# Starting addresses and group lengths of split weights in a two-layer decoder trunk

## The chip, the cores and the metric

The kernel runs on one core of one Trainium2 chip. The metric is the time of one execution on the device, in microseconds: before the change 1123.68 us as the median of three runs (1123.16 to 1127.1).

## The reference: what is computed

A trunk of two decoder layers works on 256 tokens of width 1,024. Each layer, cut to what matters here:

```python
h = rms_norm(x, norm_mix_pre[l])
q, k, v, lru_x, lru_gate, glu_in, gate_logits = split(h @ w_in[l])
y_a = dilated_attention_mixer(q, k, v, cos, sin, w_o_attn[l])   # three groups of 8 heads, rotary q and k
y_b = rg_lru_mixer(lru_x, lru_gate, ...)                        # conv(4), scan, gelu gate, w_o_lru
y_c = conformer_conv_mixer(glu_in, ...)                         # GLU, conv(31), layer norm, w_o_conv
x = x + rms_norm((g0 * y_a + g1 * y_b + g2 * y_c) @ w_out[l], norm_mix_post[l])
u = square(relu(rms_norm(x, norm_mlp_pre[l]) @ w_mlp_up[l]))    # 1024 -> 4096
x = x + rms_norm(u @ w_mlp_down[l], norm_mlp_post[l])           # 4096 -> 1024
```

All of it is fp32. All the weights are used once, so some 200 MB of them pass through the core in one execution.

## The kernel before, in words

**Split matmuls.** A product of two fp32 matrices is made of three products of rounded parts (type fp32r): high by high, high weight by low activation, low weight by high activation. Names say which: `whi_`/`wlo_` are the high and low part of a weight chunk, `hh`/`hl` (also `uh`/`ul`, `yh`/`yl`, `zh`/`zl`, `oh`/`ol`, `mh`/`ml`) those of activations.

**Chunks.** The weights come as 92 chunks of 1 MB a layer (128 partitions by 2,048 fp32). `weights()` (L508) does one: a DMA on SP's queue into `raw` (ring of 2), a cast on ScalarE that makes `whi` (L416, two pieces of 1,024 columns), a subtraction on VectorE that makes `wlo` (L429, two pieces). `whi` and `wlo` are rings of three tiles each (`NHI`). `Shifted` puts the data some elements into its tile; `off` is that offset.

**Two kinds of use.** In a "ws" chunk the weights are loaded and 256 columns of activations (all tokens) move: glu, lx, lg, q, k, ga, gb, gc, oa, ob, oc and up. A half chunk is eight row blocks k of 128, so 16 matmuls on `whi` and 8 on `wlo`; a chunk has 48. In an "as" chunk the activations are loaded and 512 columns of weights move: v, wo (w_out), ua (the first part of up) and dn (down); a chunk has 24. The chunk dn61 of layer 0 is split into separate slots (`spread`) because it is used later.

**Order.** The program is a list of operations, put in order on each engine by a list scheduler (`Sched.run`) from costs, latencies and priorities. The `main` operations, which are groups of matmuls, follow each other on TensorE in the order of the table `ORDER`; all other work of TensorE (transposes `tp`, scores `sc`, attention output `pv`, norms) is put between two of them. So a group of matmuls that is one `main` operation is not interrupted. `ws_items` (L724) gives the matmuls of a half chunk in two groups, which `ws_mm` hands to `main`; `attn_out` (L1086) calls it with four row blocks rather than eight. The scores `sc` have one PSUM tile: a score operation waits until VectorE has taken masked maxima `mx` (L969) of the one before. All matmuls are issued at L476.

**Addresses.** They follow from the tile sizes. A tile of a weight ring is (2,048 + 32) x 4 = 8,320 bytes, which is 32 x 256 + 128. Going round the ring of three, the start of a tile within 256 bytes is 128 or 0 in turn. With the offset of 64 bytes (ws chunks, v1, v2) a chunk has its high part at 192 and its low part at 64, or the other way round; with offset 0 (the other as chunks) the two are at 128 and 0, or 0 and 128. The activations' parts and the slots of dn61 all start at 128.

Of the kernel before, what the change touches and what calls it, by code (L numbers as in the profile page):

```python
# [8 lines left out]
F32R = mybir.dt.float32r  # L9
# [4 lines left out]
P = 128  # L14
# [5 lines left out]
CHUNK = 2048  # L20
# [26 lines left out]
def chunk_plan():  # L47
    q0, k0, v0, lx0, lg0, gl0, br0 = 0, 1536, 3072, 4608, 5632, 6656, 8704
    plan = []

    def ws(name, mat, c0, c1=None):
        plan.append((name, "ws", mat, (c0, c0 + P if c1 is None else c1)))

    for n in ORDER:
        kind, a = n[:2], n[2:]
        if n[0] == "v":
            for kb in range(2):
                plan.append((f"{n}{kb}", "as", "w_in", (kb, v0 + int(n[1]) * 512)))
        elif n[0] in "qk":
            plan.append((n, "rope", "w_in", (q0 if n[0] == "q" else k0) + int(n[1]) * 512 + int(n[2]) * 256))  # L60
        elif kind == "gl":
            ws(n, "w_in", gl0 + int(n[3]) * P, gl0 + D + int(n[3]) * P)
        elif kind == "oa":
            plan.append((n, "oa", "w_o_attn", int(a) * 512))
        elif kind != "lw":
            mat, c0 = {"lx": ("w_in", lx0), "lg": ("w_in", lg0), "ga": ("w_in", br0), "gb": ("w_in", br0 + D),
                       "gc": ("w_in", br0 + 2 * D), "ob": ("w_o_lru", 0), "oc": ("w_o_conv", 0)}[kind]
            ws(n, mat, c0 + int(a) * 256)
    for c in range(2):
        for kb in range(2):  # L70
            plan.append((f"wo{c}{kb}", "as", "w_out", (kb, c * 512)))
    for kb in range(9):
        if kb == 0:
            plan += [(f"ua{k}", "as", "w_mlp_up", (k, 0)) for k in range(2)]
        elif kb < 8:
            ws(f"up{2 * kb}", "w_mlp_up", (2 * kb) * 256)
            ws(f"up{2 * kb + 1}", "w_mlp_up", (2 * kb + 1) * 256)
        if kb > 0:
            for c in range(2):
                plan.append((f"dn{kb - 1}{c}", "as", "w_mlp_down", (kb - 1, c * 512)))  # L80
    return plan
# [11 lines left out]
NHI = 3  # L93
# [10 lines left out]
LINE = 128  # L104
# [272 lines left out]
def trunk_kernel(ctx: ExitStack, tc: tile.TileContext, x_d, pos_d, w_d, lruw_d, par_d, gain_d, const_d, id_d, out_d):  # L377
    nc = tc.nc
    cp = ctx.enter_context(tc.tile_pool(name="cp", bufs=1))
    wp = ctx.enter_context(tc.tile_pool(name="wp", bufs=1))  # L380
    sp = ctx.enter_context(tc.tile_pool(name="sp", bufs=1))
    pp = ctx.enter_context(tc.tile_pool(name="pp", bufs=1, space=bass.MemoryType.PSUM))
    S = Sched()
# [4 lines left out]
    def slot(name, dt=F32, shape=(P, 2, T)):  # L388
        return S.buf(sp, shape, dt, "s2", name, NSLOT)
# [58 lines left out]
    def dma(eng, out, in_, nbytes):  # L448
        def fn():
            o = out.ap() if isinstance(out, View) else out  # L450
            i = in_.ap() if isinstance(in_, View) else in_
            eng.dma_start(out=o, in_=i)

        e = {id(nc.gpsimd): "POOL", id(nc.scalar): "ACT"}.get(id(eng), "SP")
        o = S.op(e, DMA_ISSUE[e], fn, views(in_), views(out))
        o.dma = nbytes / DMA_RATE / 1e3
        return o
# [40 lines left out]
    def split(hi, lo, src, scale=None):  # L498
        if scale is None:
            return act(hi, src, AF.Copy), tt(lo, src, hi.f32(), OP.subtract)  # L500
        return (act(hi, src, AF.Copy, scale=scale),
                stt(lo, src, scale, hi.f32(), OP.mult, OP.subtract))

    KIND = {p[0]: p[1] for p in chunk_plan()}
# [3 lines left out]
    def weights(l, name, spread=False):  # L508
        c = CIDX[name]
        assert c == used[l], (name, c, used[l])  # L510
        used[l] += 1
        nm = f"{name}_{l}"
        raw = S.buf(wp, (P, CHUNK), F32, "raw", f"raw_{nm}", NRAW)
        if l or c:
            o = dma(nc.sync, raw.all(), w_d[l * NCH + c], CHUNK * P * 4)
            if l == 0 and c in late:
                S.follow(o, late[c])
        else:
            for s in range(2):
                o = dma(nc.sync, raw[:, s * HALF:(s + 1) * HALF], w_d[0][:, s * HALF:(s + 1) * HALF], HALF * P * 4)  # L520
                if ORDER[0][0] == "v":
                    S.follow(o, x1_load)
        if spread:
            hs, ls = [], []
            for q in range(4):
                hs.append(slot(f"whi_{nm}{q}", F32R, (P, 512)))
                ls.append(slot(f"wlo_{nm}{q}", F32R, (P, 512)))
                for o in split(hs[q].all(), ls[q].all(), raw[:, q * 512:(q + 1) * 512]):
                    o.prep = True
            return [(Quarters(hs[2 * s:2 * s + 2]), Quarters(ls[2 * s:2 * s + 2])) for s in range(2)]  # L530
        off = 0 if KIND[name] == "as" and name[:2] not in ("v1", "v2") else LINE // 8
        hi = Shifted(S.buf(wp, (P, CHUNK + LINE // 4), F32R, "whi", f"whi_{nm}", NHI), off)
        lo = Shifted(S.buf(wp, (P, CHUNK + LINE // 4), F32R, "wlo", f"wlo_{nm}", NHI), off)
        n = HALF if l == 0 and c < 2 else PREP
        for b in range(0, CHUNK, n):
            for o in split(hi[:, b:b + n], lo[:, b:b + n], raw[:, b:b + n]):
                o.prep = True
        return [(Part(hi, s * HALF), Part(lo, s * HALF)) for s in range(2)]
# [184 lines left out]

    def ws_items(ps, j, w, rhs, nk=8, pitch=P, off=0):  # L724
        hi, lo = w
        a, b = [], []
        for k in range(nk):
            s = slice(k * pitch + off, k * pitch + off + P)
            mh, ml = rhs(k)
            a.append((ps[:, j, :], hi[:, s], mh, k == 0, False))  # L730
            a.append((ps[:, j, :], hi[:, s], ml, False, False))
            b.append((ps[:, j, :], lo[:, s], mh, False, k == nk - 1))
        return a, b

    def ws_mm(ps, w, rhs):
        first = last_main[0]
        for j in range(2):
            main(*ws_items(ps, j, w[j], rhs))

    for l in range(L):  # L740
# [49 lines left out]
        def glu(i):  # L790
            w = weights(l, f"glu{i}")
            ps = mm_ps(f"glu{i}_{l}")
            gemm(f"glu{i}", w, ps, hr)
            if i % 2 == 0:
                upad[i // 2] = S.buf(sp, (P, 2, 288), F32, "upad", f"upad{i}_{l}", 4)
                memset(upad[i // 2][:, :, 0:30], 0.0)
            u2 = upad[i // 2]
            th = slot(f"gth{i}_{l}", shape=(P, T))
            act(th.all(), ps[:, 1, :], AF.Tanh, scale=0.5)
            stt(u2[:, i % 2, 30:30 + T], th.all(), 1.0, ps[:, 0, :], OP.add, OP.mult)  # L800
            if i % 2 == 1:
                conv_pair(i // 2)
# [3 lines left out]
        def lx(j):  # L806
            w = weights(l, f"lx{j}")
            ps = mm_ps(f"lx{j}_{l}")
            gemm(f"lx{j}", w, ps, hr)
            xp = S.buf(sp, (P, 2, 260), F32, "xp", f"xp{j}_{l}", 2)  # L810
            memset(xp[:, :, 0:3], 0.0)
            act(xp[:, :, 3:3 + T], ps.all(), AF.Copy)
            u = slot(f"lu{j}_{l}")
            for s in range(2):
                i = 2 * j + s
                act(u[:, s, :], ps[:, s, :], AF.Identity, scale=p1(par, CW + 24 + i), bias=p1(par, CB + i))
            for k in range(3):
                for s in range(2):
                    i = 2 * j + s
                    stt(u[:, s, :], xp[:, s, k:k + T], p1(par, CW + k * 8 + i), u[:, s, :], OP.mult, OP.add)  # L820
            lu[j] = u
            luh[j] = slot(f"luh{j}_{l}", F32R)
            lul[j] = slot(f"lul{j}_{l}", F32R)
            split(luh[j].all(), lul[j].all(), u.all())
# [3 lines left out]
        def lg(j):  # L828
            w = weights(l, f"lg{j}")
            ps = mm_ps(f"lg{j}_{l}")  # L830
            gemm(f"lg{j}", w, ps, hr)
            q = slot(f"gq{j}_{l}")
            act(q.all(), ps.all(), AF.Square, scale=0.044715 ** 0.5)
            stt(q.all(), q.all(), 1.0, ps.all(), OP.add, OP.mult)
            act(q.all(), q.all(), AF.Tanh, scale=0.7978845608028654)
            g = slot(f"gel{j}_{l}")
            stt(g.all(), q.all(), 1.0, ps.all(), OP.add, OP.mult)
            gel[j] = g
# [247 lines left out]
        mh, ml = {}, {}  # L1086
# [23 lines left out]
        for name in ORDER:  # L1110
            kind, a = name[:2], name[2:]
# [46 lines left out]
        for t in range(2):  # L1158
            nm = f"pm{l}{t}"
# [82 lines left out]
        for t in range(2):  # L1242
            nm = f"pd{l}{t}"
# [100 lines left out]
```

## Time and profile before

| | before |
|---|---|
| median of three runs | 1123.68 us |
| the profiled execution, its own time | 1124.8 us |
| its span | 1123.0 us |
| TensorE busy (matmuls) | 1103.7 us, 98% |
| VectorE busy | 903.7 us, 80% |
| ScalarE busy | 726.0 us, 65% |
| GpSimd busy | 70.8 us, 6% |
| DMA, mean over the span | 187 GB/s |

The own time is that of the whole execution; the span runs from the first to the last instruction in the trace, and all points in time below count from its start. Busy time of matmuls is a sum over a pipelined engine whose ends are modelled: the duration of a single row (0.28 us) overlaps the next, so the pace is read from one start to the next, or from the chain, where a stretch is divided by its count. Layer 0 runs to about 562 us; its MLP begins near 386. In layer 1 the MLP begins near 938.

### The profile page before, as it was taken

What the parts mean: (1) busy time and instruction counts of PE and PEld (TensorE: products, weight loads), DVE (VectorE), ACT (ScalarE), POOL (GpSimd) and SP (SyncE); (2) the same over time, 40 slices, a digit from 0 to 9 for tenths busy, and PEclk for the clock granted to TensorE, in tenths of its full rate; (3) what the DMA queues carried; (4) which work ended last, traced back from release to release, by engine and by line L of the source; (5) the groups of instructions that cost most, each with busy time, mean ns of one, the idle gap of its engine ahead of it and who ended that gap; (6) DMA issues with size and microseconds to landing.
All of it is one profiled execution on the core that took longest, in us unless ns stands there. A gap on an engine that the chain in (4) does not pass through costs nothing.

```text
span 1123.0 us, 20583 instructions
## 1 busy us (share of the span) xinstructions
PE 1103.7 (98%) x8258; PEld 1027.6 (92%) x8258; DVE 903.7 (80%) x1380; ACT 726.0 (65%) x1184; POOL 70.8 (6%) x156
## 2 busy tenths in 40 slices
PE   7999998999999999999999999999999999999997
PEld 6999998999999889988889999989989998988996
DVE  6999999999969875555679999999997789655554
ACT  5879938588765554444569897469766656444443
POOL 1000021111000010000000000221200001000000
PEclk9999999999999999999999999999999999999999
DMA  8654365655255555555556553765634365655551
GB/s 293 245 208 151 146 219 205 215 165 174 99 186 188 214 199 189 208 193 182 201 188 205 190 179 121 255 216 170 214 124 151 117 240 185 212 192 185 190 203 52
DMA packets 37649, 209.76 MB, mean 187 GB/s; under 512 B 6449, under 2 KB 9777, under 8 KB 14130
## 3 DMA queue, kind: packets, MB, share of 16 engines
q1 hardware_dynamic: 32976, 200.05, 50.7%
q0 software_dynamic: 4576, 8.40, 2.2%
q8 instruction: 65, 1.06, 0.4%
q14 instruction: 30, 0.25, 0.1%
q10 hardware_dynamic: 2, 0.00, 0.0%
HBM read 201.08 MB, written 1.05 MB: 180 GB/s over the span
## 4 chain that ended last, share of the span: by engine, by line
PE 82%; DVE 9%; DMA 4%; ACT 3%; issue 1%; SPq 1%; DVEq 0%; POOL 0%; ACTq 0%
PE dn L476 15%; PE up L476 14%; PE glu L476 8%; PE v L476 5%; PE gc L476 4%; PE wo L476 4%; PE lx L476 4%; PE oc L476 4%; PE lg L476 4%; PE k L476 3%; PE ga L476 3%; PE ob L476 2%; PE ua L476 2%; PE oa L476 2%; PE gb L476 1%; DMA qk<-r1q 1%
## 5 line engine op out<-in xcount | busy, mean ns | idle before, releaser
L429 DVE TENSOR_TENSOR wlo_dn<-raw_dn,whi_dn 128x1024 fp32r<-128x1024 f32 (+1 forms) x66 | 75.8, 1190 | 68.4 <-ACT whi_dn L416 68.4
L416 ACT CAST whi_dn<-raw_dn 128x1024 fp32r<-128x1024 f32 (+1 forms) x66 | 64.4, 1022 | 75.6 <-PE dn L476 44.0
L433 DVE SCALAR_TENSOR_TENSOR c<-upad,parh,c 128x256 f32<-128x256 f32 x256 | 110.5, 479 | 0.1
L476 PE MATMUL up<-hh_mlp,whi_up 128*128 128x256 f32 x448 | 106.3, 278 | 0.0
L476 PE MATMUL up<-hl_mlp,whi_up 128*128 128x256 f32 x448 | 106.0, 278 | 0.0
L476 PE MATMUL dn<-wlo_dn,uh 128*128 128x512 f32 x256 | 100.5, 393 | 0.0
L476 PE MATMUL dn<-whi_dn,uh 128*128 128x512 f32 x256 | 100.4, 392 | 0.0
L429 DVE TENSOR_TENSOR wlo_up<-raw_up,whi_up 128x1024 fp32r<-128x1024 f32 x56 | 66.4, 1222 | 39.1 <-ACT whi_up L416 39.1
L423 ACT ACTIVATE cpd<-upad,parh 128x256 f32<-128x256 f32 x224 | 94.6, 500 | 4.1 <-DVE c L429 4.1
L476 PEld LDWEIGHTS up<-hl_mlp,whi_up 128*128 128x128 f32 x448 | 84.3, 188 | 0.6
L476 PEld LDWEIGHTS up<-hh_mlp,whi_up 128*128 128x128 f32 x448 | 84.2, 188 | 0.6
L416 ACT CAST whi_up<-raw_up 128x1024 fp32r<-128x1024 f32 x56 | 56.2, 1048 | 36.4 <-PE dn L476 17.4
L476 PE MATMUL dn<-whi_dn,ul 128*128 128x512 f32 x256 | 70.8, 392 | 0.0
L429 DVE TENSOR_TENSOR cpd<-cpd 128x1024 f32<-128x1024 f32 (+2 forms) x84 | 63.5, 775 | 0.9 <-ACT cpd L423 0.9
L476 PE MATMUL up<-hh_mlp,wlo_up 128*128 128x256 f32 x448 | 60.7, 278 | 0.0
L476 PE MATMUL glu<-hl_mix,whi_glu 128*128 128x256 f32 x256 | 59.6, 276 | 0.0
L476 PE MATMUL glu<-hh_mix,whi_glu 128*128 128x256 f32 x256 | 59.6, 276 | 0.0
L476 PEld LDWEIGHTS dn<-whi_dn,ul 128*128 128x128 f32 x256 | 48.0, 188 | 10.8
L476 PEld LDWEIGHTS dn<-wlo_dn,uh 128*128 128x128 f32 x256 | 48.0, 188 | 10.3
L476 PEld LDWEIGHTS dn<-whi_dn,uh 128*128 128x128 f32 x256 | 48.1, 188 | 10.3
L476 PEld LDWEIGHTS up<-hh_mlp,wlo_up 128*128 128x128 f32 x448 | 55.7, 188 | 0.0
L476 PEld LDWEIGHTS glu<-hl_mix,whi_glu 128*128 128x128 f32 x256 | 48.0, 188 | 0.0
(309 smaller groups left out, 3388.3 us busy)
## 6 DMA issues: line engine op xcount, KB each, us to landing
raw_dn<-w_in_stream SPq DMA_DIRECT2D x32, 1024.0 KB, 4.8
raw_up<-w_in_stream SPq DMA_DIRECT2D x28, 1024.0 KB, 4.8
raw_glu<-w_in_stream SPq DMA_DIRECT2D x16, 1024.0 KB, 4.9
raw_q<-w_in_stream SPq DMA_DIRECT2D x12, 1024.0 KB, 4.8
raw_k<-w_in_stream SPq DMA_DIRECT2D x12, 1024.0 KB, 4.8
raw_v<-w_in_stream SPq DMA_DIRECT2D x11, 1024.0 KB, 4.9
raw_lx<-w_in_stream SPq DMA_DIRECT2D x8, 1024.0 KB, 4.8
raw_lg<-w_in_stream SPq DMA_DIRECT2D x8, 1024.0 KB, 4.8
```

Source lines behind the costliest of these rows:

```text
L416: nc.scalar.copy(out.ap(), in_.ap())
L423: nc.scalar.activation(out.ap(), in_.ap(), func, scale=val(scale), **kw)
L429: lambda: nc.vector.tensor_tensor(out=out.ap(), in0=a.ap(), in1=b.ap(), op=op), [a, b], [out])
L433: lambda: nc.vector.scalar_tensor_tensor(out=out.ap(), in0=a.ap(), scalar=val(s), in1=b.ap(), op0=op0, op1=op1), [a, b] + views(s), [out])
L476: nc.tensor.matmul(out.ap(), lhsT=lhs.ap(), rhs=rhs.ap(), start=start, stop=stop)
```

## The change

Two things are changed. First, the offsets, and with them the tiles: the high part of a ws chunk is put 192 bytes into its tile and the low part 64, v1 and v2 have both at 192, the other as chunks keep 0, and a tile has 64 spare elements rather than 32, so 8,448 bytes. Second, `ws_items` gives a half chunk with eight row blocks in four groups rather than two: the high part of four row blocks (8 matmuls), their low part (4), then the same for the other four. `ws_mm` and `attn_out` are as before; each group is one `main` operation.

```diff
-        off = 0 if KIND[name] == "as" and name[:2] not in ("v1", "v2") else LINE // 8
-        hi = Shifted(S.buf(wp, (P, CHUNK + LINE // 4), F32R, "whi", f"whi_{nm}", NHI), off)
-        lo = Shifted(S.buf(wp, (P, CHUNK + LINE // 4), F32R, "wlo", f"wlo_{nm}", NHI), off)
+        offs = (3 * LINE // 8, LINE // 8) if KIND[name] != "as" else (3 * LINE // 8,) * 2 if name[:2] in ("v1", "v2") else (0, 0)
+        hi = Shifted(S.buf(wp, (P, CHUNK + LINE // 2), F32R, "whi", f"whi_{nm}", NHI), offs[0])
+        lo = Shifted(S.buf(wp, (P, CHUNK + LINE // 2), F32R, "wlo", f"wlo_{nm}", NHI), offs[1])
...
     def ws_items(ps, j, w, rhs, nk=8, pitch=P, off=0):
         hi, lo = w
-        a, b = [], []
-        for k in range(nk):
-            s = slice(k * pitch + off, k * pitch + off + P)
-            mh, ml = rhs(k)
-            a.append((ps[:, j, :], hi[:, s], mh, k == 0, False))
-            a.append((ps[:, j, :], hi[:, s], ml, False, False))
-            b.append((ps[:, j, :], lo[:, s], mh, False, k == nk - 1))
-        return a, b
+        out = []
+        for k0 in range(0, nk, 4):
+            a, b = [], []
+            for k in range(k0, k0 + 4):
+                s = slice(k * pitch + off, k * pitch + off + P)
+                mh, ml = rhs(k)
+                a.append((ps[:, j, :], hi[:, s], mh, k == 0, False))
+                a.append((ps[:, j, :], hi[:, s], ml, False, False))
+                b.append((ps[:, j, :], lo[:, s], mh, False, k == nk - 1))
+            out += [a, b]
+        return out
```

`LINE` is 128, and a tile's element has 4 bytes: `LINE // 8` is 64 bytes, `3 * LINE // 8` is 192.

The order of the instructions on TensorE changes in every ws chunk. This is the first half chunk of lx1 in layer 0; in a row, out is left of the arrow, then moving and loaded operand (numbers are those of buffers), and x4 means four alike.

```order
 L476 MATMUL lx1_0_280<-hh_mix0_0_132,whi_lx1_0_220 128x256
 L476 MATMUL lx1_0_280<-hl_mix0_0_140,whi_lx1_0_220 128x256
+L476 MATMUL lx1_0_280<-hh_mix0_0_132,wlo_lx1_0_235 128x256 x4
 L476 MATMUL lx1_0_280<-hh_mix0_1_142,whi_lx1_0_220 128x256
 L476 MATMUL lx1_0_280<-hl_mix0_1_162,whi_lx1_0_220 128x256
```

```order
 L476 MATMUL lx1_0_280<-hh_mix0_1_142,whi_lx1_0_220 128x256
 L476 MATMUL lx1_0_280<-hl_mix0_1_162,whi_lx1_0_220 128x256
-L476 MATMUL lx1_0_280<-hh_mix0_0_132,wlo_lx1_0_235 128x256 x4
 L476 MATMUL lx1_0_280<-hh_mix0_1_142,wlo_lx1_0_235 128x256 x4
 L476 MATMUL lx1_0_280<-hh_mix0_0_132,whi_lx1_0_220 128x256
```

The four low matmuls of the first four row blocks move from behind all 16 high ones to behind the first 8; those of the other four stay.

Also on TensorE, in the attention part of layer 0: the first two scores (sc00 and sc01), which the scheduler puts between groups of the chunks gb1 and q11. Before:

```order
1031 L476 MATMUL gb1_0_2198<-hl_mix0_1_162,whi_gb1_0_2105 128x256
1032 L476 MATMUL sc00_0_2255<-qk00_0_2074 128x256 x2
1033 L476 MATMUL sc00_0_2255<-qk01_0_2002 128x128 x2
1034 L476 MATMUL sc00_0_2255<-qk02_0_2115 128x128 x2
1035 L476 MATMUL gb1_0_2198<-hh_mix0_0_132,wlo_gb1_0_2125 128x256 x4
1036 L476 MATMUL gb1_0_2198<-hh_mix0_1_142,wlo_gb1_0_2125 128x256 x4
1037 L476 MATMUL q11_0_2287<-hh_mix0_0_132,whi_q11_0_2182 128x256
...
1052 L476 MATMUL q11_0_2287<-hl_mix0_1_162,whi_q11_0_2182 128x256
1053 L476 MATMUL sc01_0_2311<-qk00_0_2074 128x256 x2
```

And now:

```order
1014 L476 MATMUL gb1_0_2200<-hl_mix0_1_162,whi_gb1_0_2091 128x256
1015 L476 MATMUL sc00_0_2228<-qk00_0_2068 128x256 x2
1016 L476 MATMUL sc00_0_2228<-qk01_0_2000 128x128 x2
1017 L476 MATMUL sc00_0_2228<-qk02_0_2113 128x128 x2
1018 L476 MATMUL gb1_0_2200<-hh_mix0_1_142,wlo_gb1_0_2123 128x256 x4
1019 L476 MATMUL gb1_0_2200<-hh_mix0_0_132,whi_gb1_0_2091 128x256
...
1035 L476 MATMUL gb1_0_2200<-hl_mix0_1_162,whi_gb1_0_2091 128x256
1036 L476 MATMUL sc01_0_2289<-qk00_0_2068 128x256 x2
```

sc00 moves from behind 40 matmuls of gb1 to behind 20, and sc01 stands 24 matmuls behind it in both.

On VectorE, the maxima of sc00 (L969 before, L972 now) at the same place, behind the low part of chunk ob1. Before:

```order
210 L429 TENSOR_TENSOR wlo_ob_0_2248<-raw_ob_0_2153,whi_ob_0_2216 128x1024 x2
211 L429 TENSOR_TENSOR c_0_493<-c_0_493,cpd_0_1734 128x256
212 L433 SCALAR_TENSOR_TENSOR c_0_786<-upad_0_85,parh,c_0_786 128x256 x2
213 L969 ISA sm_0_2280,mx_0_2281<-sc_0_2255,const 128x512
214 L969 ISA mx_0_2281 128x1
```

And now:

```order
215 L429 TENSOR_TENSOR wlo_ob_0_2237<-raw_ob_0_2151,whi_ob_0_2214 128x1024 x2
216 L972 ISA sm_0_2258,mx_0_2259<-sc_0_2228,const 128x512
217 L972 ISA mx_0_2259 128x1
218 L972 ISA sm_0_2268,mx_0_2269<-sc_0_2228,const 128x512
219 L972 ISA mx_0_2269 128x1
220 L429 TENSOR_TENSOR c_0_485<-c_0_485,cpd_0_1762 128x256
```

The additions of the convolution, which stood between `wlo_ob` and the maxima, now stand behind them.

## Rows read from the trace of the kernel before

**Rows 1.** The page: span, busy time (share, instructions) and the chain's shares.
```profile
span 1123.0 us, 20583 instructions
PE 1103.7 (98%) x8258; PEld 1027.6 (92%) x8258; DVE 903.7 (80%) x1380; ACT 726.0 (65%) x1184; POOL 70.8 (6%) x156
...
PE 82%; DVE 9%; DMA 4%; ACT 3%; issue 1%; SPq 1%; DVEq 0%; POOL 0%; ACTq 0%
```

**Rows 2.** The chain, ws stretches: start us, us, what, count.
```profile
30.41 27.20 PE glu L476 x240
...
341.77 21.76 PE oc L476 x192
...
421.47 11.31 PE up L476 x96
...
443.85 10.90 PE up L476 x96
...
465.76 11.08 PE up L476 x96
...
649.20 11.31 PE lg L476 x96
```

**Rows 3.** Windows: us, busy time (count) by engine, granted clock (PEclk), DMA.
```profile
172.00:183.00 11.00, 7.86 (x59) 7.29 (x58) 9.99 (x18) 9.89 (x20) 2.12 (x5) 0.84 0.62 212
...
398.00:562.00 164.00, 164.00 (x1051) 148.13 (x1051) 94.79 (x108) 81.82 (x111) 3.68 (x4) 1.00 0.55 194
...
715.00:883.00 168.00, 165.18 (x1376) 154.65 (x1375) 149.38 (x266) 117.86 (x214) 22.28 (x45) 1.00 0.55 183
```

**Rows 4.** Timeline of PE, up from 465.59: start us, us, operation, count.
```profile
465.59 0.28 PE L476 MATMUL up<-hh_mlp,whi_up 128*128 128x256 f32 x1
...
468.42 0.28 PE L476 MATMUL up<-hh_mlp,whi_up 128*128 128x256 f32 x1
...
470.30 1.09 PE L476 MATMUL up<-hh_mlp,wlo_up 128*128 128x256 f32 x8
471.23 0.28 PE L476 MATMUL up<-hh_mlp,whi_up 128*128 128x256 f32 x1
```

**Rows 5.** Timeline of PE, oa of layer 0: first, and 48 matmuls later.
```profile
330.44 0.28 PE L476 MATMUL oa<-oh,whi_oa 128*128 128x256 f32 x1
...
336.10 0.28 PE L476 MATMUL oa<-oh,whi_oa 128*128 128x256 f32 x1
```

**Rows 6.** The chain, as stretches.
```profile
363.53 20.73 PE wo L476 x90
...
410.41 11.06 PE dn L476 x48
```

**Rows 7.** Timeline of PE, first half of dn61: first, and 12 matmuls later.
```profile
548.62 0.39 PE L476 MATMUL dn<-whi_dn,uh 128*128 128x512 f32 x1
...
551.34 0.40 PE L476 MATMUL dn<-whi_dn,uh 128*128 128x512 f32 x1
```

**Rows 8.** Waits of PE: for what: us in total, times, longest us.
```profile
PE sc L476 <- DVE mx L969: 4.8, 2, 3.1
...
PE tp L483 <- ACT sm L423: 1.2, 1, 1.2
...
PE sc L476 <- DMA qk<-r1k: 0.5, 1, 0.5
```

**Rows 9.** The chain where q20 of layer 0 begins.
```profile
140.41 1.23 DVE wlo_q L429
...
141.68 3.90 PE q L476 x32
```

**Rows 10.** Timeline of DVE ahead of the first maxima (idle before in brackets).
```profile
174.19 2.36 DVE L429 TENSOR_TENSOR wlo_ob<-raw_ob,whi_ob 128x1024 fp32r<-128x1024 f32 x2 [1.01 <-ACT whi_ob L416]
176.47 0.42 DVE L429 TENSOR_TENSOR c<-c,cpd 128x256 f32<-128x256 f32 x1
...
177.59 0.68 DVE L969 CUSTOM_DVE_ANT_0 sm<-sc,const 128x512 f32<-128x512 f32 x1
```

## The prediction

> **What bounds the kernel now.** I read the page first [rows 1]. TensorE is busy 1103.7 of 1123.0 us, and the chain of work that ended last runs over it for 82%. The profiled execution took 1124.8 us, 1.8 more than its span; the median of the three runs is 1123.68, so a sum made against the profiled one is set 1.1 us lower for the forecast. With TensorE full, the time changes if a matmul gets shorter or longer, or if an idle gap comes or goes.
>
> The chain comes next, because its PE rows hold long stretches of one kind, and a stretch divided by its count is the pace of a matmul. For the "ws" chunks, where 256 columns of activations move [rows 2], there are two paces for one and the same shape: 27.20 / 240 and 21.76 / 192 are 113.3 ns, but 11.31 / 96 is 117.8. The pairs of up chunks in the MLP show 11.31, 10.90 and 11.08 for equal work, so the pace goes with something other than the operation. The clock is not it: it is full in 398 to 562 us [rows 3]. The addresses do go with it. From the allocation one works out where each high and low tile starts within 256 bytes: the tiles are 8,320 bytes, an odd multiple of 128, so in a ring of three the start alternates, and a high/low pair is at 192/64 or at 64/192. The three kinds of up pairs, which come round in turn, are just these: 11.31 where both chunks are at 192/64, 11.08 where the first is at 64/192 and the second at 192/64, and 10.90 the other way round.
>
> The timeline inside such a pair shows how the pace changes [rows 4]. The pair at 465.76 in the chain begins with a chunk at 64/192. (Its first matmul starts at 465.59; the chain counts from when the one before has ended.) The first 16 + 8 matmuls are slow (465.59 to 468.42: 2.83 us for 24, 117.9 ns), and so are the next 16 (468.42 to 470.30: 117.5). With the low group of 8 it begins to run quicker (470.30 to 471.23: 116), and the pair's 11.08 says that the rest is quick: 96 x 113.3 and 40 to 48 times 4.5 ns more are 11.06 to 11.09. The slow pace is no even 117.8 but a cycle of three starts, about 120, 120 and 113 ns apart. Going through the stretches in this way I find a rule that covers most of them: the slow pace is entered after something that is not ws (down projection, transposes, gates); it ends only where a group at 64 is followed by one at 192, and then only if the group ends at the right place of the cycle. A group of n that begins p places into the cycle stays slow if n - 1 - p leaves 1 when divided by 3. After dn it begins at p = 2: 16 stays. After a change 192 to 64 it begins at 0: 16 leaves, 8 stays. The last is seen where oa0 repeats groups of 8 and 4 [rows 5]: 330.44 to 336.10 is 5.66 us for 48, 117.9 ns, without an exit in four repeats.
>
> For the "as" chunks, where 512 columns of weights move, chain rows give 11.06 / 48 = 230.4 and 20.73 / 90 = 230.3 ns [rows 6]. Only dn61 of layer 0, whose weights lie in separate slots, is quicker: 548.62 to 551.34 is 2.72 us for 12, 226.7 ns [rows 7]. Its high and low parts both start at 128 within 256, as the activations do; those of the others alternate between 128 and 0.
>
> **Part 1: the addresses.** Tiles of 8,448 bytes are 33 x 256, so the start no longer alternates: ws becomes 64 for high and 192 for low in every chunk (base 128 plus the offset), and as is 128 for both. v1 and v2 become 64 for both. No instruction is added.
>
> As: dn, wo and ua are 768 + 192 + 96 = 1,056 matmuls, less the 24 of dn61, 1,032. If they go from about 230.2 to dn61's 226.7 and the beginning of each chunk still takes some of its old pace (I take 227.3), that is 1,032 x 2.9 ns = 3.0 us. v, 288 matmuls, has fewer stretches at 128; I take 0.5. Bounds: 0, if dn61 is quick for another reason (slots, or one row block at a time), and 1,320 x 3.5 = 4.6. A loss I exclude, since dn61 is the same operation at the same addresses.
>
> Ws in the MLP: the twelve pairs on the chain are four at 11.31, four at 11.07 or 11.08 and four at 10.89 or 10.90, 133.1 us [rows 2]. See part 2 for what they become.
>
> **Part 2: the groups.** Each half chunk is 8 high, 4 low, 8 high, 4 low. (The first piece of order in the section on the change shows it at lx1.) By the rule, up enters after dn at p = 2 with a group of 8: 8 - 1 - 2 = 5 leaves 2, so it goes quick after 8 matmuls. A pair then costs 96 x 113.3 + 8 x 4.5 = 10.92 us, twelve cost 131.0, gain 2.1. If it doesn't leave, each is 11.31: 135.7, a loss of 2.6. These are the bounds.
>
> Ws outside the MLP: before, about 900 of 4,600 are slow by the timeline's starts, such as the 96 of lg at 649.20 [rows 2], worth 4.1 us. Other PE work (transposes, scores, gates) is a reason to enter, and almost all of it now stands ahead of a group of 4 low. Following the new order by the rule gives 700 to 900 slow; I take a gain of 0.6. Bounds: +4.1 (none slow) and -3 (the 8/4 rhythm of oa0 in all of ga, gb, gc and ob that carry insertions, 700 matmuls more x 4.5).
>
> **Waits.** PE's waits are few: 4.8 us for the maximum of the scores, 1.2 for a softmax before a transpose, 0.5 for a rotary transfer [rows 8]. The low part is needed 8 matmuls earlier, 8 x 113.3 = 0.9 us. In the MLP, VectorE is busy 95 of 164 us and ScalarE 82 [rows 3], so it hides there. In the attention part it doesn't wholly: the first low half of q20 begins at 140.41 and takes 1.23, and q goes on at 141.68 [rows 9]. I take 0.5 us of new waits there; bounds 0 and 3, the length of the longest that PE has.
>
> The scores: PE now reaches sc00 after 20 matmuls of gb1, not 40 (the rows on sc00 and sc01 in that section), and sc01 24 later as before. It comes 20 x 113.3 = 2.27 us earlier. What it waits for is the maximum (L969), itself behind wlo_ob, which begins at 174.19 when ScalarE has cast what the transfer brought [rows 10]; that is tied to the transfer, not to PE. Now the maximum stands straight behind wlo_ob (the rows on VectorE there), ahead of the 177.59 - 176.47 = 1.1 us of additions. So sc01 starts 1.1 us earlier while its engine is there 2.3 earlier: wait 3.1 becomes about 4.2, and 1.1 us of position is lost. During this wait the granted clock is 0.84 in the mean of 172 to 183 us [rows 3]; that stays. A later wait for the maximum (the other 1.7 of 4.8) has 30 rows rather than 21 between the two scores and should go mostly: -0.8. Waits in sum: 0.5 + 1.1 - 0.8 = +0.8.
>
> **Sum.** -3.0 - 0.5 - 2.1 - 0.6 + 0.8 = -5.4 on 1124.8 gives 1119.4; less 1.1, 1118.3. I say 1118.5.
>
> **Rivals.** *A, the lock (slower).* The rhythm 8/4 is that in which oa0 never left the slow pace [rows 5]. If up and the front part enter at p = 0, or the place after as at 128 is not the one seen in the old rhythm, then all chunks stay slow until something else interrupts: glu, lx and up, and pieces elsewhere, some 3,500 matmuls rather than 1,500. That is 2,000 x 4.5 = +9.0; with the gain of as (-3.5) and the waits (+0.8) +6.3, 1130. For it: rows 5. Against: after dn the groups seen begin at p = 2 four times of four. The place: the first 16 matmuls of up; it decides if a pair takes 11.3.
>
> *B, the paces don't come from the addresses, or what is won on PE is given back to transfers and VectorE.* For it: the weight stream sets parts of the attention stretch, where DVE is at 149 of 168 us [rows 3]. Then only the MLP, at most, gains (its dn and up are 3 to 4 us), waits take 2 to 3, and the time is 1122 to 1124. [...]
>
> *C, more.* Every entry leaves after one group, as is at 226.7 throughout and the new waits come to nothing: -4.1 - 2.1 - 4.6 = -10.8, so 1112.9. For it: as at 128 is exactly dn61's case. Against: transposes and scores still stand inside the chunks.
>
> **Chances.** Forecast 0.50 (own range 1115.5 to 1121.5), A 0.14, B 0.23, C 0.13. Half a per cent, 5.6 us, is about what a measurement here can tell from no change: faster is below 1118.1. Of the forecast nearly half lies below it, and all of C: 0.24 + 0.13, with some of B's low end 0.40. Slower, above 1129.3, is most of A: 0.11. The same: 0.49. The range 1112 to 1127 leaves out a part of C and the upper part of A.
>
> **What would show it.** On the chain after: up x96 at 10.9 each (right) or 11.3 (A); dn x48 at 10.9 (227) or still 11.0 to 11.1 (B); oc x192 still at 21.76; the wait for the maximum around 176 us at 4 us with the second one gone. The forecast is wrong if the sum of the up rows doesn't fall, or if new waits on DVE or DMA in 90 to 364 and 715 to 883 us come to more than 3 us.

## The result, and the profile after

The changed kernel takes 1116.92 us as the median of four runs (1113.95 to 1117.78), the one before 1123.91 beside it (1123.16 to 1127.1): ratio 0.9922, 95% interval 0.9899 to 0.9945, so 6 to 11 us faster. Run again on another occasion it took 1116.53 against 1122.63 (0.9950, 0.9932 to 0.9968, so 4 to 8 us). The forecast was 1118.5, range 1112 to 1127. The two ratios put the gain between half a per cent and 0.8%; the forecast of 0.5% lies at the lower end.

The profiled execution after is the fastest of the four: 1113.95 us, span 1112.2. So the two profiles differ by more (10.8) than the medians (7.0), and the first thing to find is which part of the 10.8 is this execution's luck. The page after, span and busy time and the chain's shares, against [rows 1]:

```profile
span 1112.2 us, 20605 instructions
PE 1095.9 (99%) x8258; PEld 1023.9 (92%) x8258; DVE 902.4 (81%) x1380; ACT 727.7 (65%) x1186; POOL 70.1 (6%) x156
...
PE 82%; DVE 10%; ACT 4%; DMA 2%; issue 1%; SPq 0%; DVEq 0%; ACTq 0%
```

TensorE's busy time falls by 7.8 us with the same 8,258 instructions, while VectorE's and ScalarE's stay within 2 us: the matmuls take less time. Not all of the 7.8 is the change's, since the sum also holds what a lower clock costs in one stretch (0.84 in the mean of 172 to 183 us before, 1.00 after); in the second profile of the changed kernel, below, the busy time is 4.3 us less than before. The chain after (start us, us, what, count), to be read against [rows 2, 6]:

```profile
30.22 27.20 PE glu L476 x240
...
336.58 21.76 PE oc L476 x192
358.35 20.43 PE wo L476 x90
...
393.33 2.31 PE up L476 x20
396.07 8.96 PE up L476 x76
405.03 10.90 PE dn L476 x48
415.93 10.92 PE up L476 x96
...
459.57 10.92 PE up L476 x96
...
642.22 10.90 PE lg L476 x96
```

Where three kinds of up pairs stood before, all twelve are now 10.92 or 10.91; dn is at 10.90 / 48 = 227.1 ns, wo at 20.43 / 90 = 227.0. What was quick before (glu, oc at 113.3) is unchanged. Only the first up pair of each layer is slow throughout: 8.96 / 76 is 117.9.

The timeline of PE in the pair that answers to [rows 4] (start us, us, operation, count):

```profile
459.41 0.28 PE L476 MATMUL up<-hh_mlp,whi_up 128*128 128x256 f32 x1
...
460.35 0.62 PE L476 MATMUL up<-hh_mlp,wlo_up 128*128 128x256 f32 x4
460.80 0.28 PE L476 MATMUL up<-hh_mlp,whi_up 128*128 128x256 f32 x1
...
461.71 0.50 PE L476 MATMUL up<-hh_mlp,wlo_up 128*128 128x256 f32 x3
```

459.41 to 460.35 is 0.94 us for 8, 117.5 ns; 460.35 to 460.80 is 0.45 for 4, and 460.80 to 461.71 is 0.91 for 8: 113. (The view ends at 462 us and so shows three of the last four.) The pace ends with the first group of 8, as the rule had it.

The waits of PE after (in total, times, longest), against [rows 8]:

```profile
PE pt_mix L483 <- DVE xn_mix L433: 3.0, 2, 2.8
PE sc L476 <- DVE mx L972: 2.2, 2, 1.4
```

And the timeline of PE, the first two scores after:

```profile
169.76 1.18 PE L476 MATMUL sc<-qk 64*128 64x256 f32 x12
174.78 1.18 PE L476 MATMUL sc<-qk 64*128 64x256 f32 x12 [0.82 <-DVE mx L972]
```

The wait that stood at 3.1 us and was forecast at 4.2 is 0.8. The second wait for the maximum stands in layer 1 and was to go mostly; it has hardly changed. Before and after:

```profile
732.60 1.18 PE L476 MATMUL sc<-qk 64*128 64x256 f32 x12 [1.64 <-DVE mx L969]
```

```profile
723.61 1.18 PE L476 MATMUL sc<-qk 64*128 64x256 f32 x12 [1.40 <-DVE mx L972]
```

Two windows after (us, busy time by engine, granted clock), for [rows 3]:

```profile
172.00:183.00 11.00, 10.18 (x89) 9.88 (x88) 11.00 (x23) 11.00 (x28) 4.90 (x11) 1.00 0.74 253
...
398.00:562.00 164.00, 163.69 (x1041) 147.58 (x1040) 95.35 (x111) 83.66 (x111) 1.99 (x4) 1.00 0.54 191
```

The granted clock is 1.00 in 172 to 183 us, where its mean was 0.84. From the first matmul of gb1 to that of ob1 it is 167.18 to 185.55 before and 167.40 to 182.12 after: this place alone gives 3.65 us of the 10.8. Without it the profiles would differ by 7.15, close to the 7.0 of the medians. Whether it belongs to the change is what the second profile of the changed kernel decides.

### The profile page after: what moved, and what is told of

Its sections match the earlier page's. It is cut to its first block, busy times and chain, and to the rows that moved or that the text cites. A ratio compares the mean times of both kernels' runs of the same rounds, so it can differ in the third digit from the quotient of the medians.

```text
span 1112.2 us, 20605 instructions
## 1 busy us (share of the span) xinstructions
PE 1095.9 (99%) x8258; PEld 1023.9 (92%) x8258; DVE 902.4 (81%) x1380; ACT 727.7 (65%) x1186; POOL 70.1 (6%) x156
## 4 chain that ended last, share of the span: by engine, by line
PE 82%; DVE 10%; ACT 4%; DMA 2%; issue 1%; SPq 0%; DVEq 0%; ACTq 0%
PE dn L476 15%; PE up L476 14%; PE glu L476 8%; PE v L476 6%; PE ga L476 4%; PE gc L476 4%; PE wo L476 4%; PE oc L476 4%; PE lx L476 3%; PE k L476 3%; PE q L476 3%; PE lg L476 2%; PE ob L476 2%; PE ua L476 2%; PE oa L476 2%; PE pv L476 1%
## 5 line engine op out<-in xcount | busy, mean ns | idle before, releaser
L476 PE MATMUL up<-hh_mlp,wlo_up 128*128 128x256 f32 x448 | 69.4, 277 | 0.0
L476 PEld LDWEIGHTS up<-hh_mlp,wlo_up 128*128 128x128 f32 x448 | 59.4, 188 | 0.0
```

The source lines that it names most:

```text
L476: nc.tensor.matmul(out.ap(), lhsT=lhs.ap(), rhs=rhs.ap(), start=start, stop=stop)
```

## The experiments

Eleven more runs were made, in three lots, each beside the kernel before on its own chip (before: 1122.63, 1122.55 and 1121.93 us). Ratios are to the kernel before of the same lot, with 95% intervals.

**Offsets only.** The diff is the first half of the change; `ws_items` stays.

> Only the offsets and tile sizes of the change, with the old groups of 16 high and 8 low, so the old order of all instructions. Theory (pace set by the addresses within 256 bytes and by the place in a cycle of three at which a group ends): dn, wo and ua go to 227 ns, a dn pair of chunks on the chain 10.90 us; up pairs enter at p = 2 with 16, stay slow for 24 matmuls, begin the second half at 0 with 16 and leave, so 40 slow and 11.06 us each (12 pairs: 132.7, only 0.4 less than before); the first wait for the maximum near 176 us keeps its length of about 3 us with half the clock behind it. Time about 1120 (-3.5 to -4.5). Rival (the groups do nothing, the addresses alone give the paces): up pairs 10.9 here too, 12 pairs 131.0, time about 1117 if the shorter wait comes from PE being faster, 1118 if not.

Measured 1118.29 us, ratio 0.9959 (0.9937 to 0.9981). The chain:

```profile
405.29 10.90 PE dn L476 x48
416.19 11.08 PE up L476 x96
...
438.17 11.08 PE up L476 x96
```

All twelve pairs are at 11.08, dn at 10.90. The theory's two numbers hold, the rival's 10.9 for up doesn't. The theory's third number fails: the wait for the maximum is 0.64 us here with the old order, and the granted clock is 1.00 in 172 to 183 us (before, it was 0.50 from 180 to 182). So the old order alone does not make the wait long.

```profile
177.09 1.18 PE L476 MATMUL sc<-qk 64*128 64x256 f32 x12 [0.64 <-DVE mx L969]
```

**Groups only.** The diff is the second half; offsets and tiles stay.

> Only the groups 8 high, 4 low, 8 high, 4 low; offsets and tile sizes of before, so the order of the changed kernel. Theory: dn and wo keep 230 ns (dn pair 11.0 to 11.1 us); the up pairs leave the slow pace after at most 12 matmuls, because 64 is followed by 192 after a group of 8 begun at p = 2 or of 4 begun at 0: 10.93 each, 12 pairs 131.2; the first wait for the maximum is shorter than 2 us and the granted clock between 172 and 183 us stays full, as in the profiled run after the change, because both come from the order. Time about 1119 (-2 from up, -3 from the wait and the clock). Rival (the wait got shorter by chance or through the faster as chunks): the wait is 3 us or more, the clock falls, and the time is 1121 to 1122.

Measured 1119.35 us, ratio 0.9970 (0.9952 to 0.9988). The chain:

```profile
407.49 11.06 PE dn L476 x48
418.55 10.95 PE up L476 x96
429.50 11.06 PE dn L476 x48
440.57 10.90 PE up L476 x96
```

dn keeps its pace of before, up has nearly that of the change (10.89 to 10.95). The two halves of the change are two effects with little in common: as comes from the offsets, up from the groups. The wait was 2.2 us, between the theory and the rival; the granted clock fell to 0.88 in the mean of 172 to 178 us and to 0.84 in that of 178 to 184, which the theory had excluded.

**The changed kernel once more**, for its second profile.

> The changed kernel once more, for the spread of its runs: its profiled run (1113.95) lay 3 us under its three others. Theory: the first wait for the maximum of the scores is near a limit; where it is about 1.4 us the clock stays full, where it is 3 or more the clock falls behind it (about 2 us more), so runs fall into two sets some 3 us apart, and this profile has either 1112 to 1114 with a clock of 1.00 in 172 to 183 us, or 1116 to 1118 with 0.84 to 0.9 there. Rival (the spread is in the first transfers): the difference of the profiles lies before 25 us, and the rest runs alike.

Measured 1116.53 us, 0.9950 (0.9932 to 0.9968), runs from 1114.33 to 1119.68. Its profiled execution took 1119.68, so 5.7 more than the first. Its busy time:

```profile
PE 1099.4 (98%) x8258; PEld 1026.9 (92%) x8258; DVE 902.5 (81%) x1380; ACT 727.7 (65%) x1186; POOL 70.2 (6%) x156
```

The timelines of PE and DVE near the second score:

```profile
169.90 1.18 PE L476 MATMUL sc<-qk 64*128 64x256 f32 x12
176.99 2.08 PE L476 MATMUL sc<-qk 64*128 64x256 f32 x12 [2.89 <-DVE mx L972]
```

```profile
173.25 2.36 DVE L429 TENSOR_TENSOR wlo_ob<-raw_ob,whi_ob 128x1024 fp32r<-128x1024 f32 x2 [0.18 <-ACT whi_ob L416]
175.53 0.69 DVE L972 CUSTOM_DVE_ANT_0 sm<-sc,const 128x512 f32<-128x512 f32 x1
```

The same program: sc00 starts at 169.76 and 169.90, but wlo_ob at 173.25, not 171.05, since the transfer of ob1 was issued 2.05 us later (166.49, not 164.44). The maxima stand behind it, so sc01 starts at 176.99 (before the change 179.04, in the first profile 174.78). The window behind the wait in the first profile of the changed kernel (us, busy time and count by engine, granted clock):

```profile
178.00:184.00 6.00, 6.00 (x53) 6.00 (x52) 5.95 (x14) 6.00 (x16) 3.80 (x8) 1.00 0.59 183
```

and in the second:

```profile
178.00:184.00 6.00, 6.00 (x35) 5.78 (x32) 5.39 (x10) 6.00 (x12) 3.60 (x8) 0.55 0.56 186
```

At a granted clock of 0.55 in the mean, after PE had waited 2.89 us, 35 matmuls start in 6 us where 53 did. Between gb1 and ob1 the second profile loses 4.8 us on the first: 2.1 of wait, and the other 2.7 with the lower clock. So the 3.65 us that the first profile won at this place can't be credited to the change: the second loses 1.2 us there against the kernel before (19.53 us from gb1 to ob1, and 18.37 before). The two sets of runs that I expected are not to be seen, though: five of the six lie from 1114.3 to 1117.0, and the sixth, the profiled one, at 1119.7. (The 1.4 us of the expectation was the wait in layer 1; at the place in question the first profile had waited 0.82.)

**High and low exchanged**: `offs = (LINE // 8, 3 * LINE // 8)` for ws, so high at 192 and low at 64.

> The changed kernel with the two ws offsets exchanged: high at 192, low at 64 within 256 bytes. Theory: behind as at 128 a group at 192 is entered at the quick pace (as the pairs of 10.90 before), so up pairs are 10.88 to 10.90 and the first pair of each layer (up2, up3), which is slow throughout in the changed kernel, is quick (-0.4 each); time 1 to 1.5 us under the changed kernel. Rival (what matters is only that high and low differ, not which is which): pairs at 10.92 as in the changed kernel, the same time within 0.5. Rival of the lock: high at 192 after as is slow and leaves only at 64 followed by 192, a group of 4 begun at 0, so after 12 matmuls: 10.93.

Measured 1115.34 us, 0.9947 (0.9928 to 0.9966). Pairs:

```profile
404.87 10.90 PE dn L476 x48
415.77 10.95 PE up L476 x96
```

Here the last of the three had it nearly: a group at 192 is entered slow behind as at 128, and the pace is left a few matmuls after the first low group of 4. The first up pair is 10.97, not 11.27. What sets the pace at the entry stays open: in the kernel before, the pairs of 10.90 also begin at 192 behind weights at 128, and those are quick from the third matmul (443.93 to 444.50 us: 0.57 for 5, 114 ns). In time this kernel isn't told apart from the changed one.

**The lock.** In the first half of the first chunk of each up pair the old group of 16 comes back:

```diff
-            main(*ws_items(ps, j, w[j], rhs))
+            main(*ws_items(ps, j, w[j], rhs, size=4 if j else size0))   # size0 = 8 for up2, up4, ..., else 4
```

> The changed kernel, but in the first of each pair of up chunks (up2, up4, ... up14) the first half chunk has the old groups of 16 high and 8 low; all other half chunks keep 8, 4, 8, 4. Theory (a group of n begun p places into the cycle of three stays slow if n - 1 - p leaves 1 divided by 3): 16 begun at 2 stays, and every group of 8 behind it begins at 0 and stays, so the whole pair is slow: 96 x 117.8 = 11.31 us, 12 pairs 135.7 and not 131.0, time +4.7 against the changed kernel, about 1121. Rival (shorter groups simply leave sooner, wherever they begin): slow for 24, then quick within the next 8 to 16: pairs 11.0 to 11.06, time +1 to +1.7.

Measured 1121.29 us, ratio 1.0001 (0.9979 to 1.0022). All twelve pairs:

```profile
417.35 11.31 PE up L476 x96
428.66 10.90 PE dn L476 x48
...
1079.65 11.31 PE up L476 x96
```

The same first half chunk of 16 and 8 gives 11.08 where the old groups follow and 11.31 where the new ones do, at the same addresses: behind it a group of 16 ends the slow pace and groups of 8 don't, although a group of 8 straight behind dn ends it in the changed kernel. So what counts is the length of a group together with where it begins, as the rule had forecast. This one edit costs the whole gain of the change.

**v1 and v2 at 128** (`(0, 0)` for all as chunks).

> The changed kernel with v1 and v2 at offset 0 like the other as chunks, so at 128 within 256 rather than 64. Theory (weights that move run quicker where they start like the loaded activations, at 128): the v1 rows of the chain go from 11.04 us for 48 to 10.90, v2's alike; in both layers some 190 matmuls x 2.9 ns = -0.5 us. Rival (what made dn, wo and ua quicker is that high and low no longer differ): v1 and v2, whose two parts are already both at 64, stay at 11.04.

Measured 1117.17 us, 0.9957 (0.9936 to 0.9978). v1 and v2 became slower, which neither foresaw:

```profile
779.11 11.21 PE v L476 x48
```

In the changed kernel it was 11.04:

```profile
774.33 11.04 PE v L476 x48
```

The loaded activations of v1 and v2 are every second token (a step of two elements), those of dn, wo, ua and v0 stand together; for the stepped operand 64 is the better of the two starts, by 0.17 us a pair of chunks.

**As at 0**: `(LINE // 4, LINE // 4)` for wo, ua and dn.

> The changed kernel with wo, ua and dn at offset 128 bytes, so both parts at 0 within 256 while the loaded activations stay at 128. Theory (like start is what is quick): dn pairs 11.2 us or more (the mean of 230.2 before was one half at 128, 226.7, and one at 0, so 233.7: 11.22), time about +4 against the changed kernel. Rival (only that both parts start alike matters): dn pairs 10.90.

One execution, 1122.62 us. dn is steady in all pairs, and slower:

```profile
407.06 11.15 PE dn L476 x48
418.20 10.93 PE up L476 x96
```

11.15 / 48 is 232.3 ns against 227.1 at 128, less than the 233.7 expected. That high and low start alike isn't enough; the start at which the loaded activations lie too, 128, is the quick one of the two.

**Maxima first.** The maxima of sc00 go ahead of ob1's low part, and sc01 behind the first group of q11:

```diff
+                    for o in lows["ob1"][-2:]:
+                        S.follow(top, o)
...
+        S.follow(starts["q11"], score_ops[1])
```

> The changed kernel with the maxima of the first score ahead of both halves of ob1's low part on VectorE, and the second score of each layer behind the first group of q11 on TensorE, so 36 and not 24 matmuls behind the first score. Theory (the wait near 176 us hangs on when ob1's transfer lands, because the maxima stand behind its low part, and that is what moves the runs by 3 to 5 us): PE's wait for the maximum there goes below 0.3 us in any run, the granted clock is 1.00 from 172 to 184 us, the runs lie within 2 us of each other but for disturbed ones, and the median is 1114 to 1115. Rival (the spread comes from elsewhere, the transfers themselves): the wait goes, but the runs spread over 3 to 5 us as before and the median is 1116 to 1117.

Measured 1117.16 us, 0.9950 (0.9934 to 0.9967), runs from 1114.47 to 1120.32. The waits:

```profile
PE g_rest L476 <- DMA g_row<-gain_in: 3.1, 1, 3.1
PE sc L476 <- DMA qk<-r1k: 2.2, 2, 1.2
...
PE sc L476 <- DVE mx L975: 0.7, 1, 0.7
```

In the one execution that was profiled the wait near 176 us is gone and the clock is full, but the runs spread as before and the median isn't lower; waits for rotary transfers come to 2.2 us, 0.5 before the change, the longest of them in layer 1. The rival has it: in the profiles this wait is one of several places that differ (the first transfers, lg1, the scores of both layers), and which of them moves a given run stays open.

**Exchanged, with the old groups.**

> The offsets exchanged (high at 192, low at 64 within 256 bytes, as at 128) with the old groups of 16 and 8, so the old order. Theory: the run with exchanged offsets showed that a group at 192 behind as at 128 is entered slow; here the only place to leave is a low group of 8 at 64, begun at 0, and 8 - 1 - 0 = 7 leaves 1: it stays. So all up pairs 11.31 us, the slow pace stays in the front part too wherever it was entered, and as gains 3.5 as before: 1121 to 1124, 5 us or more over the changed kernel. Rival (the address pair alone decides, and 8/4 or 16/8 is the same): pairs 10.95 as with the exchanged offsets and groups of 8 and 4.

Measured 1126.64 us, ratio 1.0042 (1.0028 to 1.0056): slower than before.

```profile
29.92 28.27 PE glu L476 x240
...
420.13 11.31 PE up L476 x96
431.44 10.94 PE dn L476 x48
```

The lock holds in front too: glu is 28.27, not 27.20, and some 4,300 ws matmuls are slow by the starts in the timeline (about 900 or 1,100 in the two profiles of the changed kernel). The time is 2.6 us over what was expected, probably since I had not counted the attention part as locked. as is quick all the same: here its gain is more than lost.

**Row block by row block**, main operations of 12 in the order high, high, low, with the exchanged offsets, and then with those of the change:

```diff
-                b.append((ps[:, j, :], lo[:, s], mh, False, k == nk - 1))
-            out += [a, b]
+                a.append((ps[:, j, :], lo[:, s], mh, False, k == nk - 1))
+            out.append(a)
```

> The exchanged offsets, and within each half chunk every row block by itself: two matmuls on the high part, one on the low part, in main operations of 12. Theory: a low group of 1 at 64, begun at 0, leaves 0 and so ends the slow pace after 3 matmuls: up pairs 10.89, fewer than 200 slow ws matmuls, -1 to -2 us on the paces against the exchanged kernel; the low part is needed 6 matmuls earlier (0.7 us) and takes back up to 1 us of it: 1114 to 1115.5. Rival (changing between two tiles at every second matmul has a price of its own): the quick pace is above 113.3 throughout, 6,000 x some ns, 1120 or more.

> The same row block order with the offsets of the change (high at 64, low at 192). Theory: a high group of 2 at 64, entered after dn at 2, leaves 2 (that is, -1) and goes quick at once: up pairs 10.89; but where it is entered at 0 it stays (2 - 1 = 1) until something interrupts, so the first up pair of each layer and parts of ga and gc are slow throughout, and the time lies between the exchanged one in this order and the changed kernel plus 1: 1115 to 1118. Rival (a group of two is too short for the rule): all pairs 11.3 or all 10.88.

Measured: exchanged 1114.53 us, 0.9929 (0.9906 to 0.9953); offsets of the change 1118.11, 0.9959 (0.9944 to 0.9973). Pairs of the one:

```profile
416.67 10.90 PE up L476 x96
```

And of the other, with the rest of the first up pair ahead of them and oc of layer 1 behind:

```profile
400.01 8.19 PE up L476 x72
...
419.10 10.89 PE up L476 x96
...
889.65 22.86 PE oc L476 x190
```

The twelve pairs behind the first are alike, as the rule has it for both. It fails at the first pair of each layer with the offsets of the change: that was to be slow throughout, and its last 72 matmuls take 8.19 us, 113.8 ns each. The difference between the two kernels lies in the attention part: some 320 slow ws matmuls in the one (fewer than 200 were expected) and some 1,470 in the other by the starts in the timeline, oc among them. 1,150 x 5.4 ns (the slow ones are 118.7 apart here) would be 6.2 us; the medians show 3.6, and what takes up the rest was not traced. The quick pace stays 113.3 (glu takes 27.20 us for 240) when the tile changes every second matmul, so that rival falls. The low part, needed sooner, brings a new wait of 1.7 us before oc with the exchanged offsets (1.6 with those of the change):

```profile
PE oc L476 <- DVE wlo_oc L429: 1.7, 2, 0.9
```

The exchanged one has the lowest median of all that ran; against the changed kernel, from another lot, the intervals overlap.

## Why the prediction was right, point by point

- **As, -3.0 and v -0.5.** Right in place and size. dn went to 227.1 to 227.2 ns where 227.3 was taken, and v takes 0.5 us less by its starts. The quick dn (10.90 to 10.94 a pair) appears in every kernel with as at 128 and in none without. What I gave as the reason (dn61 is quick because it starts where the activations do) holds for contiguous activations against a start at 0, and fails for v1 and v2.
- **Up pairs, -2.1.** The number is right to the digit: 10.92 forecast, 10.92 measured. The rule that carries it was read from a handful of stretches, and it was then tested where it forecasts a loss (the lock, 11.31) and where it forecasts nothing from the old groups (11.08). Over the starts of all thirteen traces, a slow group at 64 that begins behind one at 192 stayed slow with 8 matmuls in 484 of 508 cases and with 2 in 353 of 361, and ended the pace with 1, 4, 16 or 24 in 138 of 143; all 24 exceptions at 8 stand behind a low group cut short by other work. Two things in the rule are not right. The cycle of three starts, about 120, 120 and 113 ns apart, is not in the trace: before the change, 1,422 of the 1,473 gaps of 117 ns or more between neighbouring ws matmuls are 117 to 119. So the place p in a cycle is a number fitted to where the pace ended, and these lengths are all that supports it. And the entry is not explained, as the exchanged offsets and the first pairs show. The first pair of each layer I had left out: it is entered after ua and the transposes, locks, and costs 0.2 and 0.35 us. With as at 0 the same pair, in the same order, took 10.91.
- **Ws elsewhere, -0.6.** By the starts in the timeline, outside the MLP some 630 and 860 are slow in the two profiles of the changed kernel, against 910 before: -1.3 and -0.2 us. The size is right, and it varies from run to run. (The ws matmuls outside the MLP are 4,800, not the 4,600 of the prediction, on which the sum doesn't rest.)
- **Waits, +0.8.** This step failed in each of its parts. For the first wait (+1.1) I read the transfer of ob1 as fixed, and derived 4.2 us from the order; it was 0.82 and 2.89 us in two executions of the changed kernel. It is the transfer that moves. By the time from the start of sc00 to the cast of ob1 on ScalarE, the waits line up: with the old order 1.3 us gave a wait of 3.15 (before) and -1.2 gave 0.64 (offsets only); with the new order 0.2 gave 0.82 and 2.3 gave 2.89 (two executions of the changed kernel), 1.1 gave 2.18 (groups only) and 1.4 gave 2.12 (exchanged). So the new order waits some 0.7 to 1.2 us less for the same lag, with only two executions to stand for the old one. That is about what the maxima's new place behind wlo_ob was to give. But the lag itself differs by 2.1 us between two executions of one program, and I had read one value of it as fixed. The second wait (-0.8) did not go: 1.64 us before, 1.40 and 1.62 after. New waits (0.5) came to 0.8 us in the first profile and 1.9 in the second. All the waits of PE that the view lists are 12.7 us before, 10.0 and 12.2 after: -2.7 and -0.5, not +0.8.
- **Rival A, the lock,** is what the mixed groups and the exchanged offsets with old groups show: all twelve pairs at 11.31, and some 4.8 us (1121.29) and 10 us (1126.64) over the changed kernel of the first lot. It doesn't decide here because the first group of 8 behind dn ended the pace in all twelve pairs on the chain.
- **Rival B.** Its first half, that the paces don't come from the addresses, the runs contradict: the same instructions in the same order took 11.31 a pair with one set of offsets (exchanged, old groups) and 11.08 with another (offsets only). Nor was the gain given back to transfers.
- **Sum.** -5.4 forecast, -7.0 and -6.1 measured in medians. The two halves alone gave -4.3 and -3.3 us by medians, 7.6 together against 6.1 for both, each with some 2 us of uncertainty. The sum came near because as and up carry it; that the failed wait term did little harm is owed to its small size and, in the first profile, to luck with that execution.

## What to carry to other kernels

When equal matmuls show two paces in the chain, write the start addresses of their operands beside them, and the order in which the tiles change, before looking for a wait. A rule found in a trace should be tested where it forecasts a loss: the kernel that puts 16 and 8 ahead of groups of 8 and 4 told more than any that got faster. And two profiles differ by what an execution happens to meet; here two executions of one program differed by 5.7 us, as much as the change was worth.

## What the runs showed of the hardware that was not expected

- Matmuls of 256 columns run at one of two paces, 117.8 or 113.3 ns, for hundreds on end (4.5 ns each: glu's 240 took 28.27 us or 27.20). The slow one was entered after other shapes, though not after each, and in unbroken stretches it was left only where weights at 64 within 256 bytes were followed by weights at 192. The cause inside TensorE is open; only the rule was tested.
- Moving 512 columns takes 227.1 ns with weights at 128 and 232.3 with weights at 0 where the loaded activations are contiguous at 128; with activations at every second token 233.5 (11.21 / 48) at 128 and 230.0 (11.04 / 48) at 64.
- After the wait near 176 us the granted clock stayed full in seven executions that waited 0.39 to 1.44 us and in one that waited 2.12 (exchanged offsets); in the mean of 178 to 184 us it was 0.84, 0.55 and 0.72 in three that waited 2.18, 2.89 and 3.15.
